# Third and fifth chunk of the feed-forward blocks by Strassen's scheme, and the gate by one Silu

## The chip, the cores and the metric

The kernel runs on one core of one Trainium2 chip. The metric is device microseconds from launch to end of one execution; lower is better. A core has TensorE (PE, matrix products, with its weight loads shown as PEld), VectorE (DVE), ScalarE (ACT), GpSimd (POOL) and SyncE (SP, which here only issues DMAs). Each engine works through its own queue in order; semaphores tie the queues together.

## The reference

Two layers of a decoder trunk, 256 tokens of width 1024, all in float32. A layer is a feed-forward half step, a mixer of three attention groups, and a second feed-forward half step:

```python
def swiglu(x, w_gate, w_up, w_down):
    return (jax.nn.silu(x @ w_gate) * (x @ w_up)) @ w_down
...
for l in range(DEPTH):
    h = h + 0.5 * swiglu(rms_norm(h, ffn1_norm[l]), ffn1_w_gate[l], ffn1_w_up[l], ffn1_w_down[l])
    h = h + hybrid_mixer(rms_norm(h, mix_norm[l]), w_in[l], ...)
    h = h + 0.5 * swiglu(rms_norm(h, ffn2_norm[l]), ffn2_w_gate[l], ffn2_w_up[l], ffn2_w_down[l])
```

The hidden width is 2816, so there are four feed-forward blocks, each with a 1024 x 2816 gate, a 1024 x 2816 up and a 2816 x 1024 down matrix. `rms_norm` scales a token by r, the inverse root of its mean square, and by a gain for each column. Since r is one number a token, the kernel multiplies it in after the product: silu(r g) * (r u), with g and u the products without r.

## The kernel before, in words

*Numbers.* Float32 products are made of three passes (`mm3`, line 391): each operand is split into a high part and the rest, and high x high, high x rest and rest x high are added up in PSUM. So one 128 x 128 x 512 product costs three matmuls, all recorded at line 389.

*Weights.* `Stream` writes down the order of all weights; the host packs them in that order. `Weights` takes them through at the kernel's run: a "raw" of 1 MB is loaded by SP (line 220) into one of 5 buffers; a "unit", half a raw, is split by a cast on ScalarE (`high`, line 278) and a subtraction on VectorE (`low`, line 282) into one of 8 pairs of buffers, `wh` and `wl`; `take` hands the oldest pair to TensorE. `pump`, called after every unit that TensorE is given, keeps the splitting up to 7 units ahead. `hold` and `free` keep new loads back while activations go to memory and return.

*A feed-forward block* (`ffn`, line 500). The hidden columns come in five chunks of 512 (the loop at line 773, c = 0 to 4, called first to fifth here) and a last half chunk of 256 gate and 256 up columns. A chunk has the gate and the up product for two tiles of 128 tokens: 8 column tiles of the input x 2 token tiles x 2 matrices x 3 passes = 96 matmuls of 512 columns. Between them stand four units (two in the fifth chunk) of the down product of the chunk before, 12 matmuls each. The gate is `gate` (line 553): a Tanh on ScalarE of r g / 2 (line 555), then (tanh + 1) * g on VectorE (line 556); `up` (line 559) multiplies by u r². The factors that are left over go into the residual sum, 0.25 at lines 536, 539 and 837. `factors` (line 758) makes r/2, r² and -r² from r, three small VectorE operations. The result is turned by VectorE, written to memory and read back (`to_memory`, `back`, lines 477 and 562), and split for the down product some steps later (`after`).

*Strassen's scheme* (`seven`, line 635). The two token tiles, the two halves of the input columns and the pair gate/up make 2 x 2 block matrices, so a chunk is 8 block products of 12 matmuls. With sums of input blocks (`seven_forms`, made once a block and spread over the steps of the first two chunks), sums of weight blocks and sums of results, 7 do. The raws r11 and r21 hold the gate's two halves, r12 and r22 the up's. In this chunk VectorE makes six sums of weight units (line 249): r12 + r22 into a tile `own`, then + r11, later + r21; GpSimd issues two DMAs that add r11 onto r12 (line 247); ScalarE copies three results out of PSUM (line 652) and VectorE adds three (lines 669, 672, 682). The chunk has 14 units instead of 16, each of its weight units is used for 6 matmuls, not 12, and its four raws are wanted almost at once. `SEVEN` (line 63) says which chunks of the four blocks go this way: the fourth in blocks 1 to 3, the third and fifth in block 4.

*After a block.* `tail` (line 839) adds the last down products, finishes the residual, and makes the next norm's input; the next block or mixer follows. Block 4 ends in `finish` (line 522). In the first block of a layer, the head gains for the mixer are loaded behind the fifth chunk (line 811).

*Tables of ScalarE.* Line 369 loads the table for Exp and Tanh at the start. The mixer's `log_sigmoid` (line 1049) goes from Exp to Ln and, with a small Exp at line 1053, back; later the mixer uses Tanh (line 1260) and Exp (line 1300).

Of the kernel before, what the change touches and what calls it, by code (L numbers as in the profile page):

```python
# [10 lines left out]
F32 = mybir.dt.float32  # L11
F32R = mybir.dt.float32r
I32 = mybir.dt.int32
AF = mybir.ActivationFunctionType
ALU = mybir.AluOpType
# [3 lines left out]
P = 128  # L19
# [40 lines left out]
MIX_START = [("iq", (0, 1, 2)), ("ib", (0,)), ("iq", (3,)), ("ib", (1, 2, 3))]  # L60
FAR = 3
GAINS_AT = 4
SEVEN = ((3,),) * 3 + ((2, 4),)
ADD_AHEAD = 4
EARLY = 1
HOLD_AT, HID_AT = 2, 4
# [234 lines left out]
def kernel(ctx: ExitStack, tc: tile.TileContext, x, xt, weights, small, const, out):  # L301
# [7 lines left out]
    sm = ctx.enter_context(tc.tile_pool(name="sm", bufs=4))  # L309
# [6 lines left out]
    V, A, G, T = nc.vector, nc.scalar, nc.gpsimd, nc.tensor  # L316
# [4 lines left out]
    def tmp(n):  # L321
        return tp.tile([P, 512], F32, name="tmp", tag="tmp")[:, :n]
# [15 lines left out]
    ones = cp.tile([P, P], F32, name="ones")  # L338
# [7 lines left out]
    def head_gains(l):  # L346
        gb = cp.tile([P, 6, HD], F32, name="gb", tag="gb")
        nc.sync.dma_start(gb, small[l])
        return gb
# [16 lines left out]
    W.n_raw_done += RAW_BUFS - 4  # L366
    W.issue(RAW_BUFS)

    A.activation(tmp(P), ones, AF.Exp)

    def load_small():
        nc.sync.dma_start(cst, const)
# [120 lines left out]
    def residual(q, ps, factor, cols=slice(0, 512)):  # L493
        t, c = q % 2, q // 2
        d = trunk[:, t, 512 * c + cols.start:512 * c + cols.stop]
        V.scalar_tensor_tensor(d, ps, factor, d, op0=ALU.mult, op1=ALU.add)  # L496
        return d


    def ffn(norm, nxt, aside=None, first=False):  # L500
        hid, due, step, own_gains = {}, [], [0], []
# [6 lines left out]
        def stepped(pumps=2):  # L508
            step[0] += 1
            for x in [x for x in due if x[0] <= step[0]]:  # L510
                due.remove(x)
                x[1]()
            W.pump(pumps)
# [8 lines left out]
        def finish(ks, early):  # L522
            ws = [(k, W.take()) for k in ks]
            dst = out[0].rearrange("(t p) d -> p t d", p=P)
            n = len(ks) - 2
            for q in range(3):
                for k, w in ws[:n]:
                    tokens(acc[q], q, hid[k], w, False, False)
                if q < len(early):
                    early[q]()  # L530
            for q in range(4):
                for c in ((0, 512),) if q < 3 else ((0, 256), (256, 512)):
                    c = slice(*c)
                    o = bank("gu")[:, :S] if c.start else acc[q][:, c]
                    if c.start:
                        residual(q, acc[q][:, c], 0.25, c)
                    for k, w in ws[n if q < 3 else 0:]:
                        tokens(o, q, hid[k], w, c.start > 0 and k == ks[0], k == ks[-1], c)
                    d = residual(q, o, 0.25, c)
                    at = 512 * (q // 2) + c.start  # L540
                    nc.sync.dma_start(dst[:, q % 2, at:at + c.stop - c.start], d)

# [9 lines left out]

        def gate(ps, t, n):
            a = tmp(n)
            A.activation(a, ps[t][:, :n], AF.Tanh, scale=hr[:, t:t + 1])  # L555
            V.scalar_tensor_tensor(a, a, 1.0, ps[t][:, :n], op0=ALU.add, op1=ALU.mult)  # L556
            return a

        def up(a, u, t):
            V.scalar_tensor_tensor(a, u, r2[:, t:t + 1], a, op0=ALU.mult, op1=ALU.mult)  # L560

        def back(k0, n, sc):
            hT = at.tile([P, 8, 32 * n], F32, name="hT", tag="kT")
# [71 lines left out]
        def seven(c):  # L635

            def piece(part, t, half):
                return [part[:, 4 * half + k, t * P:(t + 1) * P] for k in range(4)]

            def form(ps, x, start, stop=False, last=False):  # L640
                hs, ls = x if isinstance(x, tuple) else forms[x]
                for u in range(2):
                    w = W.take()
                    for k in range(2):
                        n = 2 * u + k
                        mm3(ps, (hs[n], ls[n]), [v[:, k] for v in w], start and n == 0, stop and n == 3)
                    if not (last and u):
                        stepped()

            def keep(ps):  # L650
                s = tmp(512)
                A.copy(s, ps)
                return s

            own = lambda t, half: (piece(norm.h, t, half), piece(norm.l, t, half))
            n_down = 1 if c == NC - 1 else 2
            y = bank("gu")
            form(y, own(0, 0), True)
            s1 = keep(y)
            x = bank("gu")  # L660
            form(x, own(0, 1), True, True)
            z = bank("gu")
            form(z, "f3", True)
            form(y, "f2", False, last=True)
            u2 = keep(y)
            stepped()
            for i in range(n_down):
                down(4 * c - 4 + i)
            V.tensor_tensor(s1, x, s1, op=ALU.add)
            form(y, "f1", False)  # L670
            u4 = keep(y)
            V.tensor_tensor(u4, z, u4, op=ALU.add)
            for i in range(n_down):
                down(4 * c - 4 + n_down + i)
            W.hold = True
            form(y, "f4", False, True)
            a0 = gate([s1, None], 0, 512)
            V.scalar_tensor_tensor(a0, y, minus_r2[:, 0:1], a0, op0=ALU.mult, op1=ALU.mult)
            sc = memory(4, "hd")
            to_memory(sc, 0, a0, 4)  # L680
            form(z, own(1, 1), False, True, True)
            V.tensor_tensor(u2, z, u2, op=ALU.add)
            a1 = gate([None, u2], 1, 512)
            V.scalar_tensor_tensor(a1, u4, minus_r2[:, 1:2], a1, op0=ALU.mult, op1=ALU.mult)
            to_memory(sc, 1, a1, 4)
            last = c == NC - 1
            if c == at_seven[-1]:
                forms.clear()
                W.home = None
            after(HID_AT, back(4 * c, 4, sc))  # L690
            W.free(1 if last else 2)
            stepped()
# [58 lines left out]
        W.home = wide().rearrange("p (a b) -> p a b", a=4)  # L751
        if first:
            g0, u0 = opening()
        hr = sm.tile([P, 2], F32, name="hr", tag="hr")
        r2 = sm.tile([P, 2], F32, name="r2", tag="r2")
        minus_r2 = sm.tile([P, 2], F32, name="minus_r2", tag="minus_r2")

        def factors():
            V.tensor_scalar(hr, norm.r, 0.5, None, op0=ALU.mult)
            V.tensor_tensor(r2, norm.r, norm.r, op=ALU.mult)  # L760
            V.tensor_scalar(minus_r2, r2, -1.0, None, op0=ALU.mult)

        if not first:
            g0, u0 = ([bank("gu") for _ in range(2)] for _ in range(2))
            for n, (ps, u) in enumerate(((g0, 0), (g0, 1), (u0, 0), (u0, 1))):
                unit(ps, u)
                if n == 1:
                    norm.sums()
                if n == 2:
                    norm.rest()  # L770
                stepped()
        acc = None
        for c in range(NC):
            if c in at_seven:
                seven(c)
                continue
            ps = [bank("gu") for _ in range(2)] if c else g0
            for u in range(0 if c else 2, 4):
                unit(ps, u)
                if u < 3:  # L780
                    stepped()
            if c == 0:
                if first:
                    W.low()
                    norm.sums_T(xT[0])
                factors()
            a = [gate(ps, t, 512) for t in range(2)]
            stepped()
            ps = [bank("gu") for _ in range(2)] if c else u0
            for u in range(0 if c else 2, 4):  # L790
                unit(ps, u)
                if u == HOLD_AT:
                    W.hold = True
                if u < 3:
                    stepped()
                if u == 1 and c:
                    acc = acc or [bank("acc") for _ in range(4)]
                    for k in range(4 * c - 4, 4 * c - (2 if c == NC - 1 else 0)):
                        down(k)
            sc = memory(4, "hd")  # L800
            for t in range(2):
                up(a[t], ps[t], t)
                to_memory(sc, t, a[t], 4)
            after(6 if c + 1 in at_seven else HID_AT, back(4 * c, 4, sc))
            W.free()
            stepped()
            if c == 1 and first:
                load_small()
            if c == 0:
                seven_forms()  # L810
            if c == GAINS_AT and aside is not None:
                own_gains.append(head_gains(aside))
# [21 lines left out]
            down(k)  # L834
        ks = list(range(4 * NC - 4, NF))
        early = (split,)
        return tail(acc, hid, ks, 0.25, nxt, None, early) if nxt else finish(ks, early)

    def tail(acc, rhs, ks, factor, make_norm, late=None, early=()):

# [695 lines left out]
```

## Time and profile before

| | |
|---|---|
| median of 3 runs | 984.07 us (983.64 to 985.1) |
| profiled execution, first to last instruction | 982.0 us |
| instructions | 13337, of them 4644 matmuls |
| weight traffic and the rest by DMA | 223.49 MB, mean 228 GB/s |
| groups of matmuls at L389 | 67% of the chain into `ps_gu` (gate, up, mixer), 31% into `ps_acc` (down, out) |
| loads of activation tables | 5, of 1283 ns each (lines 369, 1052 twice, 1053 twice) |

No other time of the profiled execution is at hand than its span; the median lies 2.1 us above it. In the profile's rows, "L389 PE MATMUL a<-b,c xN | busy, mean ns | idle before" is a group of instructions of one line, engine and operation; "x <- y" in a wait says that x waited until y ended. The span of an operation is its latency: consecutive matmuls overlap, and so do, by less, consecutive operations of VectorE and ScalarE. TensorE's clock is given as granted by the throttle.

### The profile page before, as it was taken

Reading aid. Unit: us, or ns where it says so; the run is one execution under the profiler, and the core shown is the slowest. Engines: PE = TensorE matmul, PEld = TensorE weight load, DVE = VectorE, ACT = ScalarE, POOL = GpSimd, SP = SyncE. Lnnn points to the kernel's source line nnn. Section 1 sums busy time; section 2 is a strip of 40 time slices with the busy share of each in tenths; the row PEclk is TensorE's granted clock in tenths of the full one; section 3 lists DMA queues with packets and bytes.
Section 4 is the critical chain, followed back from the end, with each engine's and each line's share of the span. In section 5 each row is a group of like instructions: output and inputs, shape, how many; then the busy total and the mean of one; then the engine's idle time right before and its main releaser. Section 6 shows DMA issues by size and latency. Waiting matters only on the chain.

```text
span 982.0 us, 13337 instructions
## 1 busy us (share of the span) xinstructions
PE 977.6 (100%) x4644; PEld 809.5 (82%) x4644; DVE 806.9 (82%) x1299; ACT 583.3 (59%) x986; POOL 163.5 (17%) x184
## 2 busy tenths in 40 slices
PE   9999999999999999999999999999999999999998
PEld 8888888888878888888888888888888788888887
DVE  6987976789987887796589779676899869998894
ACT  6753853567786654555475437546777855575561
POOL 0000002278530000000000000040867200000000
PEclk9999999999999999999999999999999999999999
DMA  9776866484554786568676668765646448686662
GB/s 343 298 285 222 298 256 219 167 303 139 206 188 134 270 274 225 164 240 295 231 266 252 225 168 305 256 222 179 254 172 219 163 140 289 188 300 245 184 250 72
DMA packets 80435, 223.49 MB, mean 228 GB/s; under 512 B 18144, under 2 KB 48112, under 8 KB 59888
## 3 DMA queue, kind: packets, MB, share of 16 engines
q1 hardware_dynamic: 76112, 213.16, 60.4%
q0 software_dynamic: 1440, 5.24, 3.0%
q10 hardware_dynamic: 2816, 4.24, 1.5%
q8 instruction: 36, 0.59, 0.2%
q14 instruction: 31, 0.25, 0.1%
HBM read 205.29 MB, written 17.33 MB: 227 GB/s over the span
## 4 chain that ended last, share of the span: by engine, by line
PE 100%; DVE 0%; POOL 0%; issue 0%; POOLq 0%
PE ps_gu L389 67%; PE ps_acc L389 31%; PE ps_gu L1317 1%; PE ps_acc L985 1%; PE ps_acc L424 0%; PE ps_acc L1317 0%; PE ps_acc L1443 0%; PE ps_gu L1443 0%; PE ps_acc L1119 0%; DVE trunk L496 0%; POOL ones L339 0%; POOL minus_half L341 0%; POOLq L1513 0%
## 5 line engine op out<-in xcount | busy, mean ns | idle before, releaser
L389 PE MATMUL ps_gu<-wh,xhl 128*128 128x512 f32 (+2 forms) x1720 | 531.2, 387 | 0.0
L282 DVE TENSOR_TENSOR wl<-raw,wh 128x1024 fp32r<-128x1024 f32 (+2 forms) x340 | 404.9, 1228 | 12.9 <-ACT wh L278 12.5
L278 ACT CAST wh<-raw 128x1024 fp32r<-128x1024 f32 (+2 forms) x340 | 341.6, 1040 | 117.9 <-PE ps_gu L389 56.8
L389 PEld LDWEIGHTS ps_gu<-wh,xhl 128*128 128x128 f32 x1720 | 321.9, 188 | 63.5 <-issue 1.0
L389 PE MATMUL ps_gu<-wl,xhl 128*128 128x512 f32 (+2 forms) x860 | 329.3, 384 | 0.0
L389 PEld LDWEIGHTS ps_gu<-wl,xhl 128*128 128x128 f32 x860 | 161.6, 188 | 30.4
L389 PE MATMUL ps_acc<-wh,hh 128*128 128x512 f32 (+1 forms) x352 | 136.7, 388 | 0.0
L389 PE MATMUL ps_acc<-wh,hl 128*128 128x512 f32 (+1 forms) x352 | 136.5, 388 | 0.0
L389 PE MATMUL ps_acc<-wl,hh 128*128 128x512 f32 (+1 forms) x352 | 136.4, 388 | 0.0
L389 PEld LDWEIGHTS ps_acc<-wl,hh 128*128 128x128 f32 x352 | 66.1, 188 | 13.8 <-DVE wl L282 0.3
L389 PEld LDWEIGHTS ps_acc<-wh,hl 128*128 128x128 f32 x352 | 66.1, 188 | 13.6
L389 PEld LDWEIGHTS ps_acc<-wh,hh 128*128 128x128 f32 x352 | 66.1, 188 | 13.5
L572 ACT CAST hh<-hT 128x256 fp32r<-128x256 f32 x88 | 29.4, 404 | 74.2 <-DMA hT<-hd 74.2
L278 ACT CAST wh<-wide 128x1024 fp32r<-128x1024 f32 x30 | 31.2, 1048 | 53.2 <-DVE wide L249 32.6
L560 DVE SCALAR_TENSOR_TENSOR tmp<-ps_gu,r,tmp 128x512 f32<-128x512 f32 (+1 forms) x38 | 25.8, 678 | 38.6 <-PE ps_gu L389 38.2
L573 DVE TENSOR_TENSOR hl<-hT,hh 128x256 fp32r<-128x256 f32 x88 | 32.4, 427 | 29.7 <-ACT hh L572 29.6
L247 POOL DMA_DIRECT2D raw<-in_weights_dram x10 | 9.1, 908 | 282.6 <-DMA raw<-in_weights_dram 277.1
L400 POOL TENSOR_TENSOR y_n<-msq,minus_half 128x2 f32<-128x2 f32 x6 | 7.9, 1314 | 241.2 <-DVE msq L399 241.2
L555 ACT ACTIVATE tmp<-ps_gu,hr 128x512 f32<-128x512 f32 (+1 forms) x38 | 22.9, 636 | 32.3 <-PE ps_gu L389 26.6
L282 DVE TENSOR_TENSOR wl<-wide,wh 128x1024 fp32r<-128x1024 f32 x30 | 36.0, 1212 | 4.7 <-ACT wh L278 4.4
L480 DVE STREAM_TRANSPOSE tmp<-tmp 128x512 f32<-128x512 f32 (+1 forms) x52 | 34.6, 669 | 1.7
L556 DVE SCALAR_TENSOR_TENSOR tmp<-tmp,ps_gu 128x512 f32<-128x512 f32 (+1 forms) x38 | 22.7, 624 | 15.8 <-ACT tmp L555 15.7
(260 smaller groups left out, 1033.3 us busy)
## 6 DMA issues: line engine op xcount, KB each, us to landing
raw<-in_weights_dram SPq DMA_DIRECT2D x160, 1024.0 KB, 6.4
hd<-tmp SPq DMA_DIRECT2D x40, 256.0 KB, 2.0
hT<-hd SPq DMA_DIRECT2D x80, 128.0 KB, 2.7
raw<-in_weights_dram POOLq DMA_DIRECT2D x10, 512.0 KB, 7.5
raw<-in_weights_dram SPq DMA_DIRECT2D x4, 768.0 KB, 7.9
raw<-in_weights_dram SPq DMA_DIRECT2D x4, 672.0 KB, 4.8
raw<-in_weights_dram SPq DMA_DIRECT2D x8, 256.0 KB, 4.6
raw<-in_weights_dram SPq DMA_DIRECT2D x4, 512.0 KB, 7.1
```

What stands on the lines that cost most here:

```text
L247: self.nc.gpsimd.dma_start(self.part(*unit), self.kept(rs[0], *unit[1:]), accum_op=ALU.add)
L278: self.nc.scalar.copy(hv, src)
L282: (engine or self.nc.vector).tensor_tensor(lv, self.srcs[self.n_low], hv.bitcast(F32), op=ALU.subtract)
L389: T.matmul(o, l, r, start=start, stop=stop, skip_group_check=True)
L480: V.transpose(o.rearrange("p (j b c) -> p b j c", j=4, b=n), x.rearrange("p (b j c) -> p b j c", b=n, j=4))
L555: A.activation(a, ps[t][:, :n], AF.Tanh, scale=hr[:, t:t + 1])
L556: V.scalar_tensor_tensor(a, a, 1.0, ps[t][:, :n], op0=ALU.add, op1=ALU.mult)
L560: V.scalar_tensor_tensor(a, u, r2[:, t:t + 1], a, op0=ALU.mult, op1=ALU.mult)
L572: A.copy(by(hh), x)
L573: V.tensor_tensor(by(hl), x, by(hh).bitcast(F32), op=ALU.subtract)
L985: T.transpose(ps[:, i * S + t * P:i * S + (t + 1) * P], xs[t][:, (j + i) * P:(j + i + 1) * P], ident)
L1317: T.transpose(b[:, j * P:(j + 1) * P], pj[i][:, j * P:(j + 1) * P], ident)
```

## The change

`SEVEN` becomes the third and fifth chunk for all four blocks. The gate becomes Silu of r g, one ScalarE operation whose scale is r itself; `up` multiplies by r u; Strassen's two final products use -r instead of -r². The three small VectorE operations of `factors` become one ScalarE operation, minus r; outside the first block, a Silu with a throw-away result is put behind the fourth unit of the block. The residual factor becomes 0.5. The first table loaded is Silu's. Since the fifth chunk now always goes through `seven`, the load of the head gains is called there too.

```diff
-SEVEN = ((3,),) * 3 + ((2, 4),)
+SEVEN = ((2, 4),) * 4
...
-    A.activation(tmp(P), ones, AF.Exp)
+    A.activation(tmp(P), ones, AF.Silu)
...
-                        residual(q, acc[q][:, c], 0.25, c)
+                        residual(q, acc[q][:, c], 0.5, c)
...
-                    d = residual(q, o, 0.25, c)
+                    d = residual(q, o, 0.5, c)
...
         def gate(ps, t, n):
             a = tmp(n)
-            A.activation(a, ps[t][:, :n], AF.Tanh, scale=hr[:, t:t + 1])
-            V.scalar_tensor_tensor(a, a, 1.0, ps[t][:, :n], op0=ALU.add, op1=ALU.mult)
+            A.activation(a, ps[t][:, :n], AF.Silu, scale=norm.r[:, t:t + 1])
             return a
 
         def up(a, u, t):
-            V.scalar_tensor_tensor(a, u, r2[:, t:t + 1], a, op0=ALU.mult, op1=ALU.mult)
+            V.scalar_tensor_tensor(a, u, norm.r[:, t:t + 1], a, op0=ALU.mult, op1=ALU.mult)
...
-            V.scalar_tensor_tensor(a0, y, minus_r2[:, 0:1], a0, op0=ALU.mult, op1=ALU.mult)
+            V.scalar_tensor_tensor(a0, y, minus_r[:, 0:1], a0, op0=ALU.mult, op1=ALU.mult)
...
-            V.scalar_tensor_tensor(a1, u4, minus_r2[:, 1:2], a1, op0=ALU.mult, op1=ALU.mult)
+            V.scalar_tensor_tensor(a1, u4, minus_r[:, 1:2], a1, op0=ALU.mult, op1=ALU.mult)
...
-        hr = sm.tile([P, 2], F32, name="hr", tag="hr")
-        r2 = sm.tile([P, 2], F32, name="r2", tag="r2")
-        minus_r2 = sm.tile([P, 2], F32, name="minus_r2", tag="minus_r2")
-
-        def factors():
-            V.tensor_scalar(hr, norm.r, 0.5, None, op0=ALU.mult)
-            V.tensor_tensor(r2, norm.r, norm.r, op=ALU.mult)
-            V.tensor_scalar(minus_r2, r2, -1.0, None, op0=ALU.mult)
+        minus_r = sm.tile([P, 2], F32, name="minus_r", tag="minus_r")
...
                 if n == 2:
                     norm.rest()
+                if n == 3:
+                    A.activation(minus_r, norm.r, AF.Silu)
                 stepped()
...
             if c in at_seven:
                 seven(c)
+                if c == GAINS_AT and aside is not None:
+                    own_gains.append(head_gains(aside))
                 continue
...
-                factors()
+                A.activation(minus_r, norm.r, AF.Copy, scale=-1.0)
...
-        return tail(acc, hid, ks, 0.25, nxt, None, early) if nxt else finish(ks, early)
+        return tail(acc, hid, ks, 0.5, nxt, None, early) if nxt else finish(ks, early)
```

## The prediction, written before the result

> **What bounds the kernel now.** The blocks of the feed-forward layers are called 1 to 4, their chunks first to fifth, "half" the last 256 columns. I read the page first: busy shares, the slices with the granted clock, and the chain that ended last.
>
> ```profile
> span 982.0 us, 13337 instructions
> PE 977.6 (100%) x4644; PEld 809.5 (82%) x4644; DVE 806.9 (82%) x1299; ACT 583.3 (59%) x986; POOL 163.5 (17%) x184
> PEclk9999999999999999999999999999999999999999
> PE 100%; DVE 0%; POOL 0%; issue 0%; POOLq 0%
> ```
>
> TensorE is on the chain of waits from one end to the other, at full clock. But its matmuls overlap, so a busy share of 100% doesn't yet say that it never starves. For that I took the waits of TensorE alone, and pieces of the chain in order of time (start, us, what, count):
>
> ```profile
> PE ps_gu L389 <- POOL minus_half L341: 1.0, 1, 1.0
> ```
> ```profile
> 56.08 21.76 PE ps_gu L389 x96
> 77.84 10.88 PE ps_acc L389 x48
> ```
>
> One wait of 1.0 us at the start is all. 96 matmuls take 21.76 us and 48 take 10.88: 226.7 ns each from start to start, though a group's mean shows 387 ns of latency. So a matmul of 512 columns that goes away is worth 0.2267 us, if the rest keeps up. What has to keep up is the splitting of the weights: ScalarE's cast (L278), then VectorE's rest (L282). The waits of all engines show that the ring of split weights is mostly full:
>
> ```profile
> ACT wh L278 <- PE ps_gu L389: 63.5, 44, 2.0
> ACT wh L278 <- DMA raw<-in_weights_dram: 19.3, 11, 4.7
> ```
>
> 44 times ScalarE waited for TensorE to give a buffer back; late weights cost it less.
>
> The trace has a twin of the change in it. Block 4 already does the third and fifth chunk by Strassen's scheme; blocks 1 to 3 only the fourth. So I cut the blocks into stages at each chunk's first matmul. Columns: stretch, length, then busy time and count of TensorE, its weight loads, VectorE, ScalarE, GpSimd; granted clock, share of the DMA engines, GB/s. First block 3, from the second chunk to its tail, then block 4:
>
> ```profile
> 515.60:548.20 32.60, 32.60 (x146) 27.00 (x145) 27.75 (x42) 17.27 (x28) 0.00 (x0) 1.00 0.71 255
> 548.20:580.80 32.60, 32.60 (x145) 27.03 (x144) 23.27 (x27) 14.70 (x18) 1.77 (x2) 1.00 0.63 194
> 580.80:611.10 30.30, 30.30 (x133) 24.81 (x132) 29.95 (x33) 20.16 (x25) 0.00 (x0) 1.00 0.78 278
> 611.10:638.30 27.20, 27.20 (x121) 22.52 (x121) 18.34 (x23) 13.95 (x18) 0.00 (x0) 1.00 0.67 243
> ```
> ```profile
> 824.70:857.30 32.60, 32.60 (x145) 27.04 (x144) 31.17 (x45) 17.14 (x28) 1.82 (x2) 1.00 0.68 212
> 857.30:887.70 30.40, 30.40 (x134) 24.86 (x134) 30.15 (x34) 20.39 (x26) 0.00 (x0) 1.00 0.77 278
> 887.70:920.30 32.60, 32.60 (x146) 26.99 (x145) 24.35 (x28) 15.85 (x20) 1.73 (x2) 1.00 0.71 226
> 920.30:945.50 25.20, 25.20 (x109) 20.15 (x108) 25.02 (x28) 17.93 (x23) 0.00 (x0) 1.00 0.68 250
> ```
>
> The counts are the program's (144, 144 or 132, 120 or 108) and one or two that lie across an edge. Two things are to be seen. A chunk by Strassen takes 2.0 to 2.3 us less than a plain one in the same place. And VectorE is then busy 99% of it (30.15 of 30.40, 25.02 of 25.20) against 67 to 75% in a plain third, fourth or fifth one: a Strassen chunk lives on the lead that VectorE has from the chunk before.
>
> **The change, part by part.** *Matmuls.* A plain chunk has 8 products of 12 matmuls, a Strassen chunk 7. Three blocks go from one such chunk to two: 36 matmuls fewer, 36 x 0.2267 = 8.2 us at most. The twin says less. Third chunk 32.60 to 30.40 (-2.2), fourth back from 30.30 to 32.60 (+2.3), fifth 27.20 to 25.20 (-2.0): -1.9 a block. The sums from second to fifth chunk for blocks 1, 2 and 4 (block 3 is its four rows above, 122.7):
>
> ```profile
> 28.70:151.50 122.80, 122.80 (x541) 101.40 (x540) 103.73 (x126) 69.55 (x94) 1.92 (x2) 1.00 0.76 270
> 337.90:460.70 122.80, 122.80 (x542) 101.41 (x541) 99.33 (x122) 66.31 (x89) 1.83 (x2) 1.00 0.71 245
> 824.70:945.50 120.80, 120.80 (x529) 99.03 (x528) 110.69 (x132) 71.31 (x96) 3.55 (x4) 1.00 0.71 240
> ```
>
> 2.0 + 2.0 + 1.9 = **5.9 us**, on TensorE, which sets the end. The other 2.3 us of the 8.2 are lost in Strassen chunks: 132 matmuls in 30.40 us are 230 ns each, not 227, and the fifth chunk of block 4 has two waits of weight loads:
>
> ```profile
> PEld ps_gu L389 <- DVE tmp L672: 0.4, 1, 0.4
> PEld ps_gu L389 <- ACT tmp L652: 0.4, 1, 0.4
> ```
>
> A rule on the price of a matmul, by itself: the Trainium skill, "TensorE: Matmul & The Clock Gate", section "Wait — 56ns, not 53.3ns?", gives 215.7 ns from start to start for 512 columns at full clock, by which the upper bound would be an estimated 7.8 us; the chain shows 226.7, and I go by the chain.
>
> *VectorE.* Groups by shape (count, busy, mean ns):
>
> ```profile
> L249 DVE TENSOR_TENSOR wide<-wide,raw 128x1024 f32<-128x1024 f32 x20 | 24.4, 1221 | 0.3
> L282 DVE TENSOR_TENSOR wl<-raw,wh 128x1024 fp32r<-128x1024 f32 x324 | 389.7, 1238 | 12.9 <-ACT wh L278 12.5
> L669 DVE TENSOR_TENSOR tmp<-ps_gu,tmp 128x512 f32<-128x512 f32 x5 | 3.4, 681 | 0.0
> L556 DVE SCALAR_TENSOR_TENSOR tmp<-tmp,ps_gu 128x512 f32<-128x512 f32 x30 | 19.4, 680 | 3.0 <-ACT tmp L555 2.9
> L555 ACT ACTIVATE tmp<-ps_gu,hr 128x512 f32<-128x512 f32 x30 | 19.1, 678 | 9.7 <-DVE r L760 5.6 <-PE ps_gu L389 4.0
> ```
>
> Each new Strassen chunk adds 6 sums of weights (6 x 1.22 = 7.3) and 3 sums of products (3 x 0.68 = 2.0) and drops 2 rests (2 x 1.24 = 2.5): +6.9, or 20.6 for three. The gate's operation at L556 goes everywhere: ten of 128x512 a block at 0.68, 27.2 in all, besides two half-wide ones a block. VectorE's total falls by 7 us or more. That buys nothing where the ring is full; it buys something where VectorE is short, which is the fifth chunk. By the count of a Strassen chunk, 108 x 0.230 = 24.8 us; the 0.4 above it, in four blocks, is 1.6 at most, nothing at least. I take half, 0.8.
>
> The price is in block 1, whose second chunk has VectorE fullest:
>
> ```profile
> 28.70:61.40 32.70, 32.70 (x146) 27.07 (x145) 32.12 (x46) 21.02 (x33) 0.00 (x0) 1.00 0.73 272
> ```
>
> 0.58 us are free. The third chunk's first sums fall due here, three of them (3 x 1.22 = 3.7); two gate operations leave this chunk and two the first (4 x 0.68 = 2.7). VectorE is 0.4 us late if all four count, 1.7 if only this chunk's do. Block 4 started as full (31.17 of 32.60) and lost nothing. Of 0, 0.4 and 1.7 I take 0.4: the first chunk's two do come ahead of it on VectorE's queue.
>
> *ScalarE.* Silu takes Tanh's place, one for one; the nearest row is Tanh's own 678 ns, and ScalarE stands at 59%, so nothing. What is new is a change of tables: tanh stood in one set with exp, since the trace shows no load between them. Round the mixer's logarithm the time line reads:
>
> ```profile
> 238.40 0.22 ACT L1051 ACTIVATE la<-la 128x16 f32<-128x16 f32 x1
> 238.64 1.28 ACT L1052 ACT_TABLE_LOAD   x1
> 239.93 0.22 ACT L1052 ACTIVATE la<-la 128x16 f32<-128x16 f32 x1
> 240.17 1.28 ACT L1053 ACT_TABLE_LOAD   x1
> 249.66 0.19 ACT L1114 ACTIVATE nf<-ps_acc 128x16 f32<-128x16 f32 x1 [1.65 <-PE ps_acc L389]
> ```
>
> If Silu lies in another set, each mixer has one more load, ahead of L1051, and blocks 2 and 4 one more, at the small Silu that the change puts behind their fourth unit: 4 x 1.28 = 5.1 us of ScalarE. Behind each stand casts, and in the mixer the emptying of the next banks. The ring hides the casts; in the mixer ScalarE idles 1.65 us just after. I take 0; the other bound is 5.1. Silu is in no row of this trace: that it shares a set with Copy and the casts I take from those running beside Exp and Ln without loads. A rule that speaks against the change, by itself: the Trainium skill, "ScalarE: Activation LUTs", "What ACT_TABLE_LOAD costs", counts 2.66 us a switch with its drain and tells authors to batch by set; four would be an estimated 10.6 us. This trace shows no drain: the load begins 0.02 us after L1051 ends, and the next activation 0.01 after the load.
>
> The scales of the gate lose three small VectorE operations on which ScalarE waited (5.6 us, row L555 above) and gain one on ScalarE; TensorE didn't wait there: 0.
>
> *DMA and queues.* Each Strassen chunk has two accumulating loads on GpSimd:
>
> ```profile
> L247 POOL DMA_DIRECT2D raw<-in_weights_dram x10 | 9.1, 908 | 282.6 <-DMA raw<-in_weights_dram 277.1 <-DVE wide L249 5.5
> ```
> ```profile
> raw<-in_weights_dram POOLq DMA_DIRECT2D x10, 512.0 KB, 7.5
> ```
>
> Six more are 6 x 0.91 us of an engine at 17% and 6 x 0.5 MB of traffic in stages whose DMA share was 0.77 and 0.68; four weight tiles are wanted at once rather than two. Those of the fifth chunk stand on GpSimd's queue ahead of the mixer's tables, but are issued in the chunk before, like block 4's. SP's order (write-back, four loads of the hidden rows, now six steps later after the second and fourth chunk and two after the third; head gains) is block 4's. 0, with the twin as witness.
>
> *Sum.* -5.9 - 0.8 + 0.4 = -6.3. The profiled span is 982.0, so 975.7; the median of the runs, 984.07, is 2.1 us above the span, and I take that for what lies around it: **977.8 us**.
>
> **The rivals.** *A. VectorE was the whole loss.* With the gate's operation gone, Strassen chunks run at a plain chunk's pace and all 36 matmuls count: -8.2, 975.9; with block 4's 0.4, 975.5. For it: 99% busy. Against: 230 ns a matmul also in the fourth chunks, which start with a long lead.
>
> *B. VectorE carries its lateness out of the fifth chunk (the slower side).* In block 4 it had 25.02 us of work there against 18.34, so it comes out some 6.7 us later, 5.3 with the two gates gone. Behind that chunk block 4 only ends; blocks 1 to 3 go on into a mixer or block, whose first weights are split during the tail. If the tail doesn't absorb it, TensorE starves there: up to 5.3 us at three junctions, 984.07 - 5.9 + 15.9 = 994; it turns the gain when more than 2.0 us a junction get through. Against it stand VectorE's own waits in block 2's tail:
>
> ```profile
> 481.59 0.76 DVE L573 TENSOR_TENSOR hl<-hT,hh 128x256 fp32r<-128x256 f32 x2 [2.07 <-ACT hh L572]
> 490.73 0.88 DVE L416 SCALAR_TENSOR_TENSOR xhl<-ps_acc,gx,xhl 128x256 fp32r<-128x256 f32 x2 [4.22 <-ACT xhl L413]
> ```
>
> It idles 6.3 us for others before the next block's splits: just more than it would be late.
>
> *C. The loads of tables come onto the path.* 984.07 - 5.9 + 5.1 = 983.3, no change that can be told. It decides if TensorE finds a bank not emptied. With the 2.66 us a switch that the Trainium skill gives in "ScalarE: Activation LUTs", "What ACT_TABLE_LOAD costs", the same rival would end at an estimated 988.8, slower; this trace's loads of 1.28 us speak for the lower figure.
>
> *D. The twin holds for half.* Block 1's third chunk gives 1.7 back, the fifth chunks of blocks 1 to 3 half of their 2.0: 984.07 - 5.9 + 1.7 + 3.0 = 982.9 at worst, 980 to 981 with one of the two.
>
> **How the numbers follow.** Forecast 0.62; A 0.14; D 0.13, of which 0.03 end above 982.1; C 0.05; B 0.06. About 0.2%, 2.0 us, is what a measurement of this kernel can tell from no change. Faster: 0.62 + 0.14 + 0.10 = 0.86; same 0.08; slower 0.06. The range goes down to A with its 0.4, 975.5, and up to D's milder end, 981.0.
>
> **What the changed profile would show.** TensorE's count falls by 36 to 4608. The stretch from second to fifth chunk takes 120.8 us or less in blocks 1 to 3; above 122 the twin has failed. No line L556 remains, and VectorE's total is below 800. Loads of tables are 9; 5 would mean that sets are shared, dozens that Silu's set lacks Copy. Waits of weight loads for VectorE or ScalarE within fifth chunks show whether the 0.8 came; in block 1's third chunk, the 0.4. Waits of TensorE in the first units behind blocks 1 to 3 would be B, and a span of the mixers longer than before would be C.

## The result, and the profile after

The changed kernel is slower: 995.91 us, median of 4 runs (993.8 to 999.06), beside 983.86 us for the kernel before (4 runs, 982.8 to 985.1). The ratio is 1.0125, 95% interval 1.0105 to 1.0146. The forecast was 977.8 with a range of 975.5 to 981.0, so even its range fell on the wrong side.

The page of the kernel after, the lines that answer to those shown of before: span, busy shares, granted clock by slice, and the chain that ended last by engine.

```profile
span 997.3 us, 13313 instructions
PE 976.8 (98%) x4608; PEld 805.8 (81%) x4608; DVE 820.3 (82%) x1284; ACT 610.3 (61%) x1024; POOL 158.0 (16%) x190
PEclk9999999999999999999899999998999999999999
PE 80%; DVE 8%; DMA 6%; issue 2%; ACT 1%; SPq 1%; ACTq 0%; DVEq 0%
```

The 36 matmuls are gone (4644 to 4608), and yet the span is 15.3 us longer. (The profiled execution is the slowest of the four, 999.06 us; the medians differ by 12.1.) TensorE's share of the chain falls from 100% to 80%, DMA stands in it with 6%, and two slices have a clock digit of 8. So TensorE now starves somewhere. Its waits say on what, and how often:

```profile
PE ps_acc L389 <- ACT hh L571: 14.6, 3, 5.6
```

Three waits, of 4.0 to 5.6 us, on the hidden rows (`hh`) of a down product. To place them, the same stages as in the prediction; first from the second chunk to the end of the fifth, blocks 1 to 4, then block 3's second to fifth chunk one by one:

```profile
28.70:150.50 121.80, 120.65 (x530) 98.91 (x529) 111.38 (x130) 74.49 (x100) 3.67 (x4) 1.00 0.76 267
342.70:463.20 120.50, 120.35 (x530) 98.99 (x529) 107.35 (x126) 71.34 (x96) 3.57 (x4) 1.00 0.71 237
525.70:646.20 120.50, 120.36 (x530) 98.95 (x529) 107.50 (x126) 70.91 (x96) 3.53 (x4) 1.00 0.73 243
840.50:961.00 120.50, 120.35 (x529) 98.95 (x528) 107.53 (x126) 71.65 (x96) 3.54 (x4) 1.00 0.70 238
```
```profile
558.30:588.30 30.00, 30.00 (x134) 24.80 (x133) 29.86 (x34) 20.86 (x27) 0.00 (x0) 1.00 0.77 276
...
620.90:646.20 25.30, 25.16 (x110) 20.12 (x109) 25.12 (x28) 17.95 (x23) 0.00 (x0) 1.00 0.69 250
```

Here the change does what was forecast: -1.0, -2.3, -2.2 and -0.3 us against the four sums of before, -5.8 together. The stage that the forecast's sum left at nothing is the tail, which follows the half chunk and two down products and ends where the next block or mixer begins. The tails of blocks 1 to 3, before and after:

```profile
167.80:184.60 16.80, 16.80 (x77) 13.90 (x76) 11.19 (x15) 5.75 (x13) 8.09 (x13) 1.00 0.50 154
477.00:493.80 16.80, 16.80 (x78) 13.90 (x77) 9.72 (x15) 5.75 (x13) 0.00 (x0) 1.00 0.53 174
654.70:671.40 16.70, 16.70 (x77) 13.86 (x76) 10.87 (x15) 5.65 (x13) 8.13 (x13) 1.00 0.53 155
```
```profile
166.80:189.50 22.70, 18.71 (x78) 14.90 (x77) 9.32 (x14) 6.25 (x13) 5.17 (x16) 0.92 0.52 175
479.50:503.90 24.40, 18.80 (x77) 15.12 (x76) 9.58 (x15) 6.68 (x14) 0.00 (x0) 0.86 0.54 186
662.50:687.30 24.80, 19.78 (x78) 15.76 (x77) 9.39 (x14) 6.43 (x13) 5.26 (x16) 0.86 0.48 160
```

5.9 + 7.6 + 8.1 = 21.6 us, with the granted clock down to 0.86. And -5.8 + 21.6 = 15.8, of which 15.3 show in the span; everything else (first chunks, half chunks, mixers) is within 0.5 us of before. The time line of TensorE shows what one tail consists of (start, duration, and in brackets the idle time before and its releaser):

```profile
484.71 0.39 PE L389 MATMUL ps_acc<-wh,hl 128*128 128x512 f32 x1
490.70 0.79 PE L389 MATMUL ps_acc<-wh,hh 128*128 128x512 f32 x1 [5.60 <-ACT hh L571]
...
494.27 0.49 PE L389 MATMUL ps_acc<-wh,hl 128*128 128x512 f32 x1
494.60 0.39 PE L389 MATMUL ps_acc<-wh,hh 128*128 128x512 f32 x1
```

A wait of 5.6 us, and behind it nine matmuls that start 0.43 us apart instead of 0.23: 3.9 us where nine take 2.0, so another 1.9 until the clock is back. 5.6 + 1.9 is nearly all of that tail's 7.6.

What does `hh` wait for? ScalarE's time line names a read from memory:

```profile
490.24 0.71 ACT L571 CAST hh<-hT 128x256 fp32r<-128x256 f32 x2 [9.37 <-DMA hT<-hd]
```

The views of DMA issues put a time on the round trip. They list the half chunk's write-back (count, KB each, median us from issue to landing), before and after:

```profile
hd<-tmp SPq DMA_DIRECT2D x8, 128.0 KB, 3.6
```
```profile
hd<-tmp SPq DMA_DIRECT2D x8, 128.0 KB, 9.2
```

A write of 128 KB that landed in 3.6 us now takes 9.2. SP's time line in block 2 shows the neighbours. Before (the half chunk's first matmul is at 460.7 us):

```profile
461.70 1.71 SPq L481 DMA_DIRECT2D hd<-tmp  x2
465.13 1.80 SPq L485 DMA_DIRECT2D hT<-hd  x4
467.02 0.87 SPq L220 DMA_DIRECT2D raw<-in_weights_dram  x2
470.98 3.04 SPq L481 DMA_DIRECT2D hd<-tmp  x2
477.70 1.80 SPq L485 DMA_DIRECT2D hT<-hd  x4
```

After (first matmul of the half chunk at 463.2 us):

```profile
465.06 4.33 SPq L481 DMA_DIRECT2D hd<-tmp  x2
471.04 1.80 SPq L485 DMA_DIRECT2D hT<-hd  x4
472.94 1.34 SPq L220 DMA_DIRECT2D raw<-in_weights_dram  x3
474.33 2.09 SPq L481 DMA_DIRECT2D hd<-tmp  x2
486.72 1.80 SPq L485 DMA_DIRECT2D hT<-hd  x4
```

The rows are in both cases: the fifth chunk's second write-back, its reads, weight loads of 1 MB, the half chunk's write-back, its reads. SP works in order: at the first reads it stands until the fifth chunk's write has landed. In a plain fifth chunk those reads go out 4.4 us after the half chunk has begun; by Strassen 7.8. The difference is VectorE's: it has turned the second token tile 2.4 us into the half chunk before (463.1 us), and 5.8 us into it after (469.0 us), because it works off rests of weights ahead of the first tile, and because the second still needs a sum, Silu and the multiplication behind its last product. What waited behind them then leaves at once: three loads instead of two, and the last ends 0.05 us ahead of the half chunk's write instead of 3.1. From the end of the write's issue to its reads pass 486.72 - 476.42 = 10.3 us instead of 477.70 - 474.02 = 3.7. Those loads are for the next block.

**Theory.** The small write-back stands behind 3 MB of weights, and TensorE waits for its return. **Rivals:** VectorE's lateness out of the fifth chunk (the prediction's B, at the same three junctions); the Silu and its tables; and, once the order on SP was seen, that SP's queue alone is the matter, not the DMA engines behind it.

### The profile page after: what moved, and what is told of

The parts are those of the page before. It is cut to its first block, busy times and chain, and to the rows that moved or that the text cites. A ratio compares the mean times of both kernels' runs of the same rounds, so it can differ in the third digit from the quotient of the medians.

```text
span 997.3 us, 13313 instructions
## 1 busy us (share of the span) xinstructions
PE 976.8 (98%) x4608; PEld 805.8 (81%) x4608; DVE 820.3 (82%) x1284; ACT 610.3 (61%) x1024; POOL 158.0 (16%) x190
## 4 chain that ended last, share of the span: by engine, by line
PE 80%; DVE 8%; DMA 6%; issue 2%; ACT 1%; SPq 1%; ACTq 0%; DVEq 0%
PE ps_gu L389 53%; PE ps_acc L389 24%; DVE wl L282 4%; DMA hd<-tmp 3%; DMA raw<-in_weights_dram 2%; DMA hT<-hd 1%; DVE wide L249 1%; SPq L485 1%; PE ps_gu L1313 1%; DVE hl L572 1%; PE ps_acc L981 1%; DVE tmp L480 1%; DVE tmp L559 1%; PE ps_acc L424 0%; ACT wh L278 0%
## 5 line engine op out<-in xcount | busy, mean ns | idle before, releaser
L389 PE MATMUL ps_gu<-wh,xhl 128*128 128x512 f32 (+2 forms) x1600 | 494.2, 386 | 0.2
L389 PEld LDWEIGHTS ps_gu<-wh,xhl 128*128 128x128 f32 x1600 | 298.9, 188 | 60.4 <-DVE tmp L671 1.9
L389 PE MATMUL ps_gu<-wl,xhl 128*128 128x512 f32 (+2 forms) x800 | 306.1, 384 | 0.0
L389 PEld LDWEIGHTS ps_gu<-wl,xhl 128*128 128x128 f32 x800 | 150.3, 188 | 28.2 <-DVE wl L704 0.2
L389 PE MATMUL ps_acc<-wh,hh 128*128 128x512 f32 (+1 forms) x352 | 139.6, 397 | 14.6 <-ACT hh L571 14.6
L278 ACT CAST wh<-wide 128x1024 fp32r<-128x1024 f32 x48 | 49.9, 1052 | 75.2 <-DVE wide L249 51.2
L247 POOL DMA_DIRECT2D raw<-in_weights_dram x16 | 14.3, 895 | 373.6 <-DVE wide L249 151.9
L282 DVE TENSOR_TENSOR wl<-wide,wh 128x1024 fp32r<-128x1024 f32 x48 | 57.5, 1212 | 2.2 <-ACT wh L278 1.9
L559 DVE SCALAR_TENSOR_TENSOR tmp<-ps_gu,y_n,tmp 128x512 f32<-128x512 f32 (+1 forms) x32 | 21.4, 668 | 29.9 <-PE ps_gu L389 23.9
L249 DVE TENSOR_TENSOR wide<-wide,raw 128x1024 f32<-128x1024 f32 x32 | 39.1, 1221 | 0.6
L389 PE MATMUL ps_gu<-wh,fp 128*128 128x512 f32 x96 | 33.6, 390 | 1.0 <-ACT tmp L651 1.0
```

Of the source, the lines that this page charges most:

```text
L247: self.nc.gpsimd.dma_start(self.part(*unit), self.kept(rs[0], *unit[1:]), accum_op=ALU.add)
L249: self.nc.vector.tensor_tensor(self.part(*unit), *(self.part(r, *unit[1:]) for r in rs), op=ALU.add)
L278: self.nc.scalar.copy(hv, src)
L282: (engine or self.nc.vector).tensor_tensor(lv, self.srcs[self.n_low], hv.bitcast(F32), op=ALU.subtract)
L389: T.matmul(o, l, r, start=start, stop=stop, skip_group_check=True)
L559: V.scalar_tensor_tensor(a, u, norm.r[:, t:t + 1], a, op0=ALU.mult, op1=ALU.mult)
```

## The experiments

All times are medians beside the kernel before on the same chip (983.31 to 983.84 us there).

**1. Silu alone, and Strassen in the third chunk only.** The first keeps the old choice of chunks, the second moves blocks 1 to 3 from the fourth to the third, fifth plain.

```diff
-SEVEN = ((2, 4),) * 4
+SEVEN = ((3,),) * 3 + ((2, 4),)      # silu_only
+SEVEN = ((2,),) * 3 + ((2, 4),)      # no_fifth
```

> The changed kernel with the old choice of chunks (the fourth in blocks 1 to 3, the third and fifth in block 4), so that Silu, its tables and the lost VectorE operation stand alone. Theory (the loss is in the tails of blocks 1 to 3: three weight loads go out just ahead of the half chunk's write-back, which then lands 9 us later): no tail is held up, 983 to 984.5 us, the same as before. Rival (ScalarE with its four more table loads is what costs): 4 or more us above before.

> The changed kernel with Strassen's scheme in the third chunk of blocks 1 to 3 and no longer in their fifth; block 4 keeps both. Theory: the fifth chunk's lateness brings the weight loads ahead of the write-back, so the tails are back at 16.8 us, and 982 to 983.5 us result, since the third chunk only takes the fourth's place. Rival (the third chunk, or Silu, does it): most of the 12 us stay.

Measured: 981.44 us, ratio 0.9979 (0.9969 to 0.9989), and 982.84, 0.9995 (0.9986 to 1.0004). All tails take 16.8 us in both. So Silu is worth 1.9 us (no gain was expected), its nine loads of tables cost nothing that shows, and the whole loss comes with the fifth chunk. What Silu gains lies in the Strassen chunks (block 3's fourth 30.3 to 29.9 us) and, in this execution, 0.8 us in the start. The second kernel loses 1.7 us of it in its span, 1.2 of them in block 1: there the third chunk by Strassen takes 31.1 us, where the fourth took 29.9.

**2. The half chunk's write on another queue.** `to_memory` issues these two writes from ScalarE's queue.

```diff
-    def to_memory(sc, t, x, n):
+    def to_memory(sc, t, x, n, eng=nc.sync):
...
-        nc.sync.dma_start(sc[t * P:(t + 1) * P], o.rearrange("p (j x) -> p j x", j=4))
+        eng.dma_start(sc[t * P:(t + 1) * P], o.rearrange("p (j x) -> p j x", j=4))
...
-            to_memory(sc, t, a, 2)
+            to_memory(sc, t, a, 2, A)
```

> The changed kernel with the half chunk's two write-backs issued from ScalarE's queue instead of SP's. Theory in its narrow form (the write-back stands behind 3 MB of weights in SP's queue of transfers): it lands in some 3 us instead of 9.2, TensorE doesn't wait in the tails, 976.5 to 979 us. In its wide form (the DMA engines are shared whatever the queue): it lands later than 4 us, and part of the loss stays. Rival (VectorE's lateness out of the fifth chunk is the cause): 995, as it was.

Measured: 989.08 us, 1.0054 (1.0039 to 1.0069); tails 22.9, 21.2 and 18.9. TensorE's waits on `hh` go from 14.6 to 7.3 us. SP's rows, and the write's row on ScalarE's time line:

```profile
472.99 1.40 SPq L220 DMA_DIRECT2D raw<-in_weights_dram  x3
483.36 2.29 SPq L485 DMA_DIRECT2D hT<-hd  x4
```
```profile
475.92 0.34 ACTq L481 DMA_DIRECT2D hd<-tmp  x1
```

The write passes the three loads on the queue, and still 483.36 - 476.26 = 7.1 us go by until it has landed and its reads go out. Of the 8.9 us that the loads cost this write (10.3 less the 1.4 without them, next), 5.7 stay: what is shared lies behind the queues. The Trainium skill says so in "DMA: Bandwidth & Descriptors": in "Queues, rings and completion order", that a DMA engine takes one queue's descriptors in order and turns between queues packet by packet, and in the table of its "Rules for kernel authors" that the queues of SP and ScalarE run on the same 16 engines. The trace agrees with both: 10.3 us in line, 7.1 beside the line.

**3. No load between the two write-backs.**

```diff
-            W.free(1 if last else 2)
+            if not last:
+                W.free(2)
```

> The changed kernel with no weight load let go between the fifth chunk's write-back and the half chunk's: the next block's first three loads follow behind. Both forms of the theory: write-back lands in 2 to 4 us, hidden rows are split in time, no wait in the tails, 976.5 to 979 us. Rival (VectorE's lateness): 995 as before, or worse since weights come later.

Measured: 984.52 us, 1.0011 (1.0001 to 1.0021). From the end of the write's issue at 471.32 us to its reads at 472.75 now pass 1.4 us, VectorE's work being what it was. But the tails still take 18.8, 20.7 and 18.1. ScalarE's time line shows why:

```profile
480.88 1.04 ACT L278 CAST wh<-raw 128x1024 fp32r<-128x1024 f32 x1 [6.38 <-DMA raw<-in_weights_dram]
481.83 0.71 ACT L571 CAST hh<-hT 128x256 fp32r<-128x256 f32 x2
```

In ScalarE's order a cast of the next block's weights stands ahead of the hidden rows, and its load was held back too long: it waits 6.4 us and `hh` behind it. So the loads can't just be late. There are two limits: no big load right ahead of the write, and each load landed before ScalarE comes to its cast.

**4. The same collision with a plain fifth chunk in blocks 1 to 3.** The kernel before, but with its loads kept back until the half chunk's two writes, and issued between them (all else untouched).

```diff
         for t in range(2):
             a = gate(ps, t, S)
             up(a, ps[t][:, S:], t)
+            if t and nxt:
+                W.free(3)
+                W.hold = True
             to_memory(sc, t, a, 2)
...
-            W.free()
+            if c < NC - 1:
+                W.free()
```

> The kernel before, with its own chunks and Tanh; only the weight loads that stood behind the fifth chunk's reads are put between the half chunk's two write-backs in blocks 1 to 3, two or three of them each time. Theory: this alone makes the second write-back land in 6 to 10 us and TensorE wait in the three tails, 4 to 8 us a tail with the slower clock behind a wait: 994 to 1006 us. Rival (it takes a Strassen fifth chunk to be late): 983 to 985 us.

Measured: 988.39 us, 1.0048 (1.0033 to 1.0064); tails 20.6, 18.2 and 17.7. The wait has the same name:

```profile
PE ps_acc L389 <- ACT hh L572: 3.7, 3, 1.9
```

Only two loads had a free buffer at that place, not three, and the loss is smaller than expected. But the cause is sufficient by itself, with the old gate and a plain fifth chunk.

**5. One load in front.** `one_load` lets one load go at the old place and holds the rest until the half chunk's reads; `one_early` sends that one load out ahead of the fifth chunk's reads instead, so that it has a head start.

```diff
             after(HID_AT, back(4 * c, 4, sc))
             W.free(1 if last else 2)
+            W.hold = last                 # one_load
...
+            if last:                      # one_early
+                W.free(1)
+                W.hold = True
             after(HID_AT, back(4 * c, 4, sc))
-            W.free(1 if last else 2)
+            if not last:
+                W.free(2)
```

> The changed kernel with one weight load left, not three, between the fifth chunk's hidden rows and the half chunk's write-back; the others follow behind. Theory (the write-back pays for the bytes that were asked for just ahead of it, and ScalarE's queue must not hold a cast that waits for a load ahead of the hidden rows' cast): write-back lands in 4 to 5 us, between 9.2 with three loads and 1.7 with none, and the cast that blocked ScalarE in the held kernel has its load; waits in the tails under 2 us in all, 977 to 980 us. Rival (order on the queues doesn't matter, VectorE's lateness out of the fifth chunk does): 990 or more.

> The changed kernel with that one load put ahead of the fifth chunk's reads of its hidden rows on SP's queue, so that it goes out while those wait, and all others behind the half chunk's write-back. Theory: write-back in some 2 us, load in time, no wait of TensorE in the tails (16.8 us each), so the 5.9 us of the stages remain: 976 to 978.5 us. Rival (VectorE's lateness): over 984.

Measured: 985.7 us, 1.002 (1.0011 to 1.0029), and 983.26, 0.9994 (0.9986 to 1.0003). The first misses its range: its write-back still takes 5.4 us to return, and TensorE waits 0.9 us for `hh`, 2.4 for `xhl` and 2.4 for the residual sum. In the second, TensorE no longer waits for `hh` and the tails are 17.1, 16.8 and 17.6: the loss of the changed kernel is gone. Yet it only gets that loss back: the 5.8 us saved in the chunks are gone too. What TensorE waits for now, and SP's rows behind the half chunk:

```profile
PE ps_gu L389 <- ACT xhl L453: 2.7, 2, 2.1
PE ps_acc L424 <- DVE trunk L496: 1.7, 1, 1.7
```
```profile
475.03 3.03 SPq L220 DMA_DIRECT2D raw<-in_weights_dram  x4
481.81 1.69 SPq L481 DMA_DIRECT2D xd<-tmp  x2
491.30 1.80 SPq L485 DMA_DIRECT2D xT<-xd  x4
```

The held loads, now four, stand ahead of the next small write-back, that of the next norm (`xd`): 491.30 - 483.50 = 7.8 us. The collision has moved one round trip on, into block 3's first chunk (26.0 us instead of 21.8) and the second mixer (its wide first part, 98.5 instead of 96.6).

**6. Both: one load early, and the write on ScalarE's queue.** The edit of `one_early`, and:

```diff
-            to_memory(sc, t, a, 2)
+            to_memory(sc, t, a, 2, A)
```

> The kernel with the early load, and the half chunk's write-backs on ScalarE's queue as well. Theory: nothing is left ahead of the write-back, so the queue adds nothing: within 1 us of the early load alone. If it is faster by more, something of SP's order was still in the way.

Measured: 983.84 us, 0.9997 (0.9988 to 1.0006), with the same waits on `xhl`. With 1 MB well ahead of it, the write's queue no longer matters.

**7. The remaining loads spread.** `spread` adds to `one_early` that only two loads go out behind the half chunk's reads, the rest behind all traffic of the next norm; `spread_act` also moves the half chunk's write.

```diff
         split = back(4 * NC, 2, sc)
-        W.free()
+        W.free(2)
+        W.hold = True
```

> The earlier-load version with one more edit: after the half chunk's reads are issued only two weight loads go out (four in the earlier-load version), and the rest wait until the next norm's write-back and its reads are queued. Theory (what costs is a small write-back that stands behind big weight loads, wherever it stands): the next norm's round trip is no longer late, block 3's first chunk comes back from 26.0 to 21.8 us and the wide part of the second mixer from 98.5 to 96.6, its tail before it from 17.6 to 16.8; the stages' saving of 5.9 us in the trace is then left whole: 976 to 978.5 us, ratio .992 to .9945, and the waits of PE on xhl and trunk are gone. Rival (the weights themselves come too late in this order, whoever waits: eleven loads between the fifth chunk's read and the next block's first write where before there were ten): PE then waits on wh, behind ACT's casts, in block 3's first chunk and the time stays at 982 to 985.

> The spread version with the half chunk's writes on ScalarE's queue as well. Theory: with one load ahead of the half chunk's write its round trip is no longer what anyone waits for, so the queue makes no difference: within 0.1% of the spread version. Rival (the one load ahead still costs in the tails): 1 us less than the spread version, shown by tails of 16.8 us in place of 17.1 to 17.6.

Measured: 991.62 us, 1.008 (1.0067 to 1.0093), and 991.41, 1.0076 (1.0065 to 1.0088): a miss, in the direction of the rival but further than it said. The norm's write did come back, its reads go out 1.7 us after it. But ScalarE:

```profile
505.09 1.99 ACT L278 CAST wh<-raw 128x1024 fp32r<-128x1024 f32 x2 [4.50 <-DMA raw<-in_weights_dram]
506.98 1.70 ACT L453 ACTIVATE xhl<-xT,gx 128x256 fp32r<-128x256 f32 x4
```

It is the second limit again: a cast waits for a load that was issued only at 498.5 us, and the norm's own casts stand behind it. TensorE waits 7.3 us for `xhl` in three places, and block 3's first chunk takes 28.2 us.

**8. One load, or two, behind the norm's write.** As `spread`, but one (`behind`) or two (`behind_two`) of the held loads go out directly behind the norm's first write, ahead of its reads.

```diff
                 if q == 1:
+                    W.free(1)             # behind_two: W.free(2)
+                    W.hold = True
                     nxt.fetch(2, 2)
```

> The spread version with one edit: one of the weight loads that it holds goes out right behind the next norm's first write-back (ahead of that norm's reads) instead of behind all of its traffic. In the spread version ScalarE's queue holds a cast of those weights ahead of the norm's own casts, the cast waits 4.5 us for a load issued at 498.5 us, and PE waits 3.7 us for xhl; a load behind the write in the queue left the fifth chunk's round trip at 1.75 us. Theory (two limits together: a write-back must have no big load right ahead of it, and each load must be in before ScalarE's queue comes to its cast): both are kept now, PE's waits on xhl are gone, the first chunk of block 3 takes 21.8 us in place of 28.2, the wide part of the mixers 96.6 in place of 98.7, and the time is 976 to 979 us, ratio .992 to .995. Rival (the fifth chunk by Strassen leaves too little room for the weights whatever the order): the wait moves once more, onto the norm's reads behind the load or the next cast, and the time stays at 983 us or more.

> As the version with one load behind the next norm's first write-back, but with two. Theory: the second load is not needed before the norm's casts, and two loads (2 MB) ahead of the norm's reads make them some 3 us later, which is about the room that they have: between the one-load version and 3 us more, 976 to 982 us. Rival (the weights are what is late, not the small transfers): the more loads early the better, under the one-load version by 1 us or more.

Measured: `behind` 979.67 us (978.25 to 980.46, 5 runs), 0.9956 (0.9943 to 0.9968); `behind_two` 981.3, 0.9977 (0.9968 to 0.9987). `behind` ends 0.7 us above its range. It beats the kernel before, the changed one and Silu alone, the last by intervals that only just don't overlap (up to 0.9968, from 0.9969). SP's rows and TensorE's longest wait:

```profile
474.49 0.93 SPq L220 DMA_DIRECT2D raw<-in_weights_dram  x2
481.61 1.69 SPq L481 DMA_DIRECT2D xd<-tmp  x2
483.41 0.37 SPq L220 DMA_DIRECT2D raw<-in_weights_dram  x1
485.04 1.80 SPq L485 DMA_DIRECT2D xT<-xd  x4
```
```profile
PE ps_gu L389 <- POOL minus_half L341: 1.0, 1, 1.0
```

The waits on `hh` and `xhl` are gone, block 3's first chunk takes 21.8 us, the wide first parts of the mixers 96.6 and 96.5; the load behind the write didn't hold it up (485.04 - 483.30 = 1.7 us). The profiled span, that of the fastest of the five runs, is 976.5, 5.5 less than before: -6.1 from second to fifth chunk over the four blocks, +1.3 in the tails (17.1, 16.8, 17.7), -0.7 elsewhere. The gain of the medians, 3.8 us, is less than that of this one execution; the interval reaches from 3.1 to 5.6 us, and 1.9 of the 3.8 are what Silu gave alone. In `behind_two` the norm's reads stand behind 2 MB, and 2.2 us come back in block 3's first chunk, as the theory expected.

The doses side by side, all in block 2, from SP's time lines (ScalarE's for the write in `write_on_act`): weight loads of 1 MB ahead of the half chunk's last write, the time from the end of their issue to the start of the next write's, and from the end of the last write's issue to its reads.

| run | loads ahead | by | round trip |
|---|---|---|---|
| held | none since the fifth chunk's reads | | 1.4 us |
| one_early | 1 | 3.5 us | 2.7 us |
| before | 2 | 3.1 us | 3.7 us |
| one_load | 1 | 0.1 us | 5.4 us |
| before_three | 2 | 1.4 us | 5.6 us |
| write_on_act | 3, other queue | 1.5 us | 7.1 us |
| after | 3 | 0.05 us | 10.3 us |

## Why the prediction was wrong

*The step that failed* is "DMA and queues", which ended in "0, with the twin as witness". The step looked at the order on SP's queue, but priced it by block 4. (The six steps that it gives to the reads are those of the split: `back` issues the reads at once, `after` delays the split alone, and behind the fifth chunk it does so by four steps in both kernels. The reads are late because the write is.) Block 4 has the same late reads: in the trace of before its fifth chunk's reads go out at 955.00, 9.5 us after its half chunk began, against 4.4 in block 2:

```profile
955.00 1.80 SPq L485 DMA_DIRECT2D hT<-hd  x4
957.67 1.64 SPq L481 DMA_DIRECT2D hd<-tmp  x2
```

But it is the last block: no weights follow it, SP's rows go from those reads straight to the half chunk's write, and the late reads push nothing in front of anything. In blocks 1 to 3 they push three loads in front of it, 21.6 us in the tails. The twin was a witness for what happens inside the block and could be none for what the block hands on. The trace of before had the rows to see it: the two loads between the write-backs in block 2, and none in block 4.

*Rival B* named the right junctions and the wrong carrier. It had VectorE come late out of the fifth chunk and the next block's splits starve TensorE. VectorE is in fact why the fifth chunk's write is late, by 3.4 us in block 2; for one, it works three rests off ahead of the first tile's final multiplication:

```profile
460.14 3.49 DVE L282 TENSOR_TENSOR wl<-raw,wh 128x1024 fp32r<-128x1024 f32 x3
463.54 0.75 DVE L677 SCALAR_TENSOR_TENSOR tmp<-ps_gu,minus_r,tmp 128x512 f32<-128x512 f32 x1
```

But no splits were late behind the block, the waits were on `hh`, and `behind` has the same VectorE work without the loss. B's 994 came near the measured time by another road, which is luck.

*Matmuls*, -5.9: right. -5.8 measured in those stages, -6.1 with the collision removed; the third and fifth chunks behave as in block 4 (30.0 and 25.3 us).

*VectorE*: the step's count was wrong. The section on the kernel says 14 units instead of 16; but a plain chunk is 96 matmuls at 12 a unit, so 8 units, and Strassen's 14 are six more, not two fewer. The groups show it (count, busy, mean ns):

```profile
L282 DVE TENSOR_TENSOR wl<-raw,wh 128x1024 fp32r<-128x1024 f32 x324 | 388.6, 1232 | 16.3 <-ACT wh L278 15.9
L282 DVE TENSOR_TENSOR wl<-wide,wh 128x1024 fp32r<-128x1024 f32 x48 | 57.5, 1212 | 2.2 <-ACT wh L278 1.9
```

324 rests of loaded weights as before, and 48 of summed ones where there were 30: 18 more in three chunks. Silu alone takes VectorE from 806.9 to 777.8 us, the three Strassen chunks add 42.5, and it ends at 820.3, not below 800. The total didn't set the time, since the ring covers it, but the forecast 0.8 in the fifth chunks was not there: 25.3 us, as block 4's 25.2. Silu's relief showed in the third and fourth ones (30.4 to 29.9).

*Block 1's third chunk*, +0.4 with 1.7 as the other end: the mechanism was right and the size off. It takes 31.2 us, 1.2 more than in the other blocks, for the reason given, VectorE's sums come late; ScalarE's time line shows the way to TensorE, which waits 1.0 us for the copy in the second row:

```profile
68.14 1.05 ACT L278 CAST wh<-wide 128x1024 fp32r<-128x1024 f32 x1 [3.57 <-DVE wide L249]
...
70.04 0.58 ACT L651 COPY tmp<-ps_gu 128x512 f32<-128x512 f32 x1
```

*ScalarE's tables*, 0: right. Nine loads of 1.28 us, as counted; mixers and first chunks keep their times, and rival C didn't happen. Rival A didn't either; of D only block 1's part came.

## What to carry to other kernels

A stage elsewhere in the trace that already has the change is a good witness for its inside; before it is used for a zero, look at what follows it on each queue, here whether the next block's loads stand behind it. A late small round trip on an ordered queue doesn't only come late: it bunches what waits behind it and sets that in front of the next small round trip. Prefetches must keep two distances, clear of the next short write-back and early enough for the in-order engine that takes them, and they can be spread into the gaps, behind a write and not ahead of it.

## What the hardware showed that was not expected

A write-back of 128 KB whose round trip takes 1.4 us took 5.4 behind one load of 1 MB issued 0.1 us earlier and 10.3 behind three, while one load with 3.5 us of head start cost 1.3 us. Another queue saved 3.2 of the 8.9 us that three loads cost. How the remaining part divides between the DMA engines and the memory was not tried.

In block 2 of the changed kernel nine matmuls behind a wait of 5.6 us started 0.43 us apart, for 3.9 us, so this wait cost 7.5. "TensorE: Matmul & The Clock Gate" of the Trainium skill, part 1, gives a window of about 3.4 us and 426.7 ns a matmul of 512 columns at the lower clock; the trace agrees with the second. The slow stretches don't have one length in these runs: 5.7 us behind block 3's wait of 5.0, and 6.1 behind a wait of 3.0 in `write_on_act`. Nor is there one length of wait at which the clock goes: behind the longest in `one_early`, 2.1 us, the matmuls started 0.34 and then 0.23 us apart, but soon behind one of 2.0 in `held` seven started 0.43 us apart.
